# Loading the mLSTM heads' stabilizer rows into buffers of their own, at the start of each head's products

## The chip, the core and the metric

The kernel runs on one core of a Trainium2 chip. The metric is the device time of one execution in microseconds (us), the median of the runs shown; lower is better. Inputs and weights are float32; every product of a weight matrix is made of three passes on TensorE (high part by high part, high by low, low by high), so that one "group" below means three matmuls.

## The reference, cut to what matters

The reference is a block of attention, retention and memory attention with a conv-FFN, followed by a second block of two layers: an mLSTM layer with a multi-scale pool branch (256 positions, 4 heads of 256), and a latent attention layer. The change is in the mLSTM layer. Per head, the chunkwise form of the reference is the same as a form over all 256 positions:

```
i_pre, log_f = gates                       # per head and position
cum = cumsum(log_f)
m   = running maximum of (i_pre - cum), at least 0      # the stabilizer row, 256 numbers per head
s[t, j] = (q_t . k_j) * exp(i_pre_j - cum_j - m_t)      # for j <= t
num = s @ v;  den = sum(s)
h = num / max(|den|, exp(-(cum + m))) * sigmoid(om)
h = rms_norm(h) * gain;  ya = (h + skip * xc) * silu(zm)
yb = pool branch
x + concat(ya, yb) @ w_out
```

## The kernel before

The kernel is one long stream of products on TensorE with its order written by hand; the instructions of the other engines are put into their queues by a planner that goes by program order and data dependences. Weights come in chunks: a DMA on SyncE's queue into one of three `raw` buffers, a cast to the high part `wh` on ScalarE (L370), the low part `wl` by subtraction on VectorE (L374), eight buffers each. A cast may run at most some 70 to 84 matmuls ahead of TensorE (`ahead`, L317).

Beside the products run generators, one per head. `tick()` advances every active generator to its next `yield`. `gemm_pair` ticks after each 8 groups (so twice), `om_product` twice, `narrow_product` and `qkv` once, `kstep` once (8 groups). `later(gen)` puts a generator into a waiting list, from which a tick takes one while fewer than two are active (`WIDTH`); `urgent(gen)` makes it active at once. So the number of yields of a generator fixes behind which product its own matmuls stand in TensorE's queue.

The mLSTM layer starts with the norm (`norm2`, urgent) and then has this order (L1359 to L1398): x, gate, output-gate and z products of head 0; `conv_in(0)`; `gate_rows` (urgent: the gates, the running maximum `mrow`, its DMA to DRAM `m_d`, and after six yields a transpose that gives `na`); products of head 1; `qkv(0)`; z of head 1; one bare `tick()`; `pool_products(0)` (two `gemm_pair`); `qkv(1)`; `om`, z and x products of head 2 with `conv_in(2)` after its x product; `out_steps(0)`, `out_steps(1)`; `tick()`; `qkv(2)`; `pool_products(1)`; products of head 3; `out_steps(2)`; `qkv(3)`; `out_steps(3)`; `pool_products(2)` and `(3)`; `out_steps(4)`, `(5)`; `drain()`; `ktail`. `qkv(h)` ends with `later(mlstm(h))`.

`out_steps(i)` multiplies one piece of `ya` or `yb` with the output weights, two `kstep` each, in the order of `AO_ORDER`: a0, b0, b1, a1, a2, b2; the last two pieces, a3 and b3, are done in `ktail`, tile pair by tile pair (a3 twice, b3 twice, for each pair). `out_steps` first ticks until its piece is ready. A piece a*h* is ready when `mlstm(h)` has ended.

`mlstm(h)` (L1241): wait for the gates; load `m_d`'s row of head h into `e[:, 0:256]` of all partitions (a DMA of GpSimd's queue, L1247); two yields; two VectorE steps that add `na` and the mask (L1250, L1252) and the exponential (L1253); two yields; the score product `sp` (L1256 to L1261) and its multiplication with `e` (L1262); one yield; the value products `np_` (L1267 to L1271), denominators, output gate, norm (L1273 to L1287); eight yields; the four transposes of the result (L1291, by the helper at L626); `y` (L1296, L1298) and its split into high (L417) and low (L421). The pool branch `pool(g)` is a generator too, with three yields and then its `pair_block` product of 4 groups.

Of the kernel before, what the change touches and what calls it, by code (L numbers as in the profile page):

```python
# [8 lines left out]
F32 = mybir.dt.float32  # L9
# [3 lines left out]
ALU = mybir.AluOpType  # L13
# [4 lines left out]
P = 128  # L18
# [205 lines left out]
def build(ctx, tc, aps, ch, wpar, wcon, out):  # L224
    nc = tc.nc
    V, A, PE = nc.vector, nc.scalar, nc.tensor
    E = ctx.enter_context
    cpool = E(tc.tile_pool(name="cpool", bufs=1))
# [8 lines left out]
    def nm(s):  # L237
        count[0] += 1
        return f"{s}_{count[0]}"
# [24 lines left out]
    def lo512(t):  # L264
        return t[:, 0:512]
# [4 lines left out]
    def sm(n, tag="sm", dt=F32, bufs=8):  # L270
        return small.tile([P, n], dt, tag=tag, name=nm(tag), bufs=bufs)
# [6 lines left out]
    def ps_product():  # L278
        product_tags.append(product_tags.pop(0))
        return ps(product_tags[-1])  # L280
# [22 lines left out]
    def C(name):  # L303
        g, o, n = wcon[name]
        return held[g][:, o:o + n]
# [94 lines left out]
    def mm3(out_, l, r, start, stop):  # L400
        mm(out_, l[0], r[0], start, False)
        mm(out_, l[0], r[1], False, False)
        mm(out_, l[1], r[0], False, stop)
# [408 lines left out]
    for u in range(4):  # L812
        nc.sync.dma_start(v3(lo512(TB[u])),
                            bass.AP(tensor=tb_d.tensor, offset=tb_d.offset + 127 + u * 2 * P * 385,
                                    ap=[[384, P], [P * 385, 2], [1, 256]]))
# [83 lines left out]
    for mult in (2.0 ** 14, 1.0):  # L899
# [4 lines left out]
        for n in range(4):  # L904
            if n < 3:
                m, e_ = np.frexp(rest)
# [12 lines left out]
    for w_ in range(2):  # L919
        for t in range(2):  # L920
            c_, s_ = cn[:, t * 32:(t + 1) * 32], sn[:, t * 32:(t + 1) * 32]
            for half in range(2):
# [4 lines left out]
                                       op0=ALU.mult, op1=ALU.mult)  # L927
# [173 lines left out]
    H = [dict() for _ in range(4)]  # L1101
# [66 lines left out]
    def pair_block(acc, c, b0, X2):  # L1168

        for j in range(2):  # L1170
            for k in range(2):
                w = c[b0 + k]
                mm3(acc[:, j * 256:(j + 1) * 256], (w[0][:, j * P:(j + 1) * P], w[1][:, j * P:(j + 1) * P]),
                    (X2[0][:, k * 256:(k + 1) * 256], X2[1][:, k * 256:(k + 1) * 256]), k == 0, k == 1)

    def qkv(h):
        c = Chunk(ch["qkv"][h])
        xm, xc = H[h]["xm"], H[h]["xc"]
        for m, n, sc in ((0, "q", 0.0625), (1, "k", 1.0)):
            acc = ps_product()  # L1180
            pair_block(acc, c, m * 2, xc)
            H[h][n] = new()
            A.activation(lo512(H[h][n]), acc, AF.Copy, scale=sc)
        tick()
        acc = ps_product()
        for t in range(2):
            for k in range(2):
                o = k * 256 + t * P
                mm3(acc[:, t * 256:(t + 1) * 256], (xm[0][:, o:o + P], xm[1][:, o:o + P]), c[4 + k], k == 0, k == 1)
        v = new()  # L1190
        vv = v3(v[:, 0:516])
        V.memset(vv[:, :, 256:257], 1.0)
        A.copy(vv[:, :, 0:256], v3(acc))
        H[h]["v"] = v
        free(xc, xm)
        later(mlstm(h))

    gates = {}
    m_d = dpool.tile([4 * 256], F32, name="m_d")

    def gate_rows(acc):
        ga, gb, gc = new(), new(), new()
        g = ga[0:64, 0:256]
        A.copy(g, acc[64:128, 0:256])
        V.tensor_tensor(g, g, acc[0:64, 0:256], op=ALU.add)
        V.tensor_tensor(g, g, N2["r12b"][0:64, 0:256], op=ALU.mult)
        V.tensor_scalar(g, g, G("bif")[0:64], None, op0=ALU.add)
        f = g[32:36]
        one = small.tile([64, 1], F32, tag="one", name="one", bufs=1)
        V.memset(one, 1.0)  # L1210
        t0 = ga[32:36, 256:512]
        V.scalar_tensor_tensor(t0, f, -1.0, f, op0=ALU.mult, op1=ALU.max)
        A.activation(t0, t0, AF.Exp, scale=-1.0)
        A.activation(t0, t0, AF.Ln, bias=one[32:36])
        lf = gb[0:4, 0:256]
        V.scalar_tensor_tensor(lf, f, 0.0, t0, op0=ALU.min, op1=ALU.subtract)
        zero = gb[0:4, 256:512]
        V.memset(zero, 0.0)
        rows = gc[:, 0:256]
        V.memset(rows, 0.0)  # L1220
        cum = gc[0:4, 256:512]
        V.tensor_tensor_scan(cum, lf, zero, 0.0, op0=ALU.add, op1=ALU.add)
        V.tensor_tensor(rows[0:4], g[0:4], cum, op=ALU.subtract)
        mrow = cpool.tile([4, 256], F32, name="mrow")
        V.tensor_tensor_scan(mrow, rows[0:4], rows[0:4], 0.0, op0=ALU.max, op1=ALU.max)
        nc.gpsimd.dma_start(bass.AP(tensor=m_d.tensor, offset=m_d.offset, ap=[[256, 4], [1, 256]]), mrow)
        V.tensor_tensor(rows[32:36], cum, mrow, op=ALU.add)
        for _ in range(6):
            yield
        pt = ps("q")  # L1230
        for t in range(2):
            PE.transpose(pt[:, t * P:(t + 1) * P], rows[:, t * P:(t + 1) * P], C("ident"))
        free(ga, gb, gc)
        p3 = pt[:, 0:256].rearrange("p (t c) -> p t c", t=2)
        na = sm(8, "na", bufs=1)
        emn = sm(8, "emn", bufs=1)
        V.tensor_scalar(na.rearrange("p (t c) -> p t c", t=2), p3[:, :, 0:4], -1.0, None, op0=ALU.mult)
        A.activation(emn.rearrange("p (t c) -> p t c", t=2), p3[:, :, 32:36], AF.Exp, scale=-1.0)
        gates.update(na=na, emn=emn)

    def mlstm(h):  # L1241
        while not gates:
            yield
        na, emn = gates["na"], gates["emn"]
        d_ = H[h]
        e = new()
        nc.gpsimd.dma_start(e[:, 0:256], bass.AP(tensor=m_d.tensor, offset=m_d.offset + 256 * h, ap=[[0, P], [1, 256]]))  # L1247
        yield
        yield
        V.scalar_tensor_tensor(e[:, 256:384], e[:, 128:256], na[:, 4 + h:5 + h], C("mmask")[:, 0:128],  # L1250
                               op0=ALU.add, op1=ALU.add)
        V.scalar_tensor_tensor(e[:, 0:256], e[:, 0:256], na[:, h:h + 1], C("mmask"), op0=ALU.add, op1=ALU.add)  # L1252
        A.activation(e[:, 0:384], e[:, 0:384], AF.Exp, scale=-1.0)  # L1253
        yield
        yield
        sp = ps("q")  # L1256
        qx, kx = ([d_[n][:, i * 256:(i + 1) * 256] for i in range(2)] for n in "qk")
        for i in range(2):
            mm(sp[:, 0:256], kx[i][:, 0:128], qx[i], i == 0, i == 1)
        for i in range(2):  # L1260
            mm(sp[:, 256:384], kx[i][:, 128:256], qx[i][:, 128:256], i == 0, i == 1)  # L1261
        V.tensor_tensor(e[:, 0:384], e[:, 0:384], sp[:, 0:384], op=ALU.mult)  # L1262
        yield
        hs = new()
        ss = sm(2, "su")
        vv = v3(d_["v"][:, 0:516])
        for t in range(2):  # L1267
            np_ = ps("q")
            mm(np_[:, 0:257], e[:, t * P:(t + 1) * P], vv[:, 0, 0:257], True, t == 0)
            if t:  # L1270
                mm(np_[:, 0:257], e[:, 256:384], vv[:, 1, 0:257], False, True)  # L1271
            den, dcol = sm(1, "den"), sm(1, "dcol")
            V.tensor_copy(dcol, np_[:, 256:257])  # L1273
            V.scalar_tensor_tensor(den, dcol, -1.0, dcol, op0=ALU.mult, op1=ALU.max)
            V.tensor_tensor(den, den, emn[:, 4 * t + h:4 * t + h + 1], op=ALU.max)
            V.reciprocal(den, den)
            hst = hs[:, t * 256:(t + 1) * 256]
            V.scalar_tensor_tensor(hst, np_[:, 0:256], den, d_["om"][:, t * 256:(t + 1) * 256],
                                   op0=ALU.mult, op1=ALU.mult)
            q = new()  # L1280
            A.activation(q[:, 0:256], hst, AF.Square, accum_out=ss[:, t:t + 1])
            free(q)
        free(e)
        r = rsqrt(mean_eps(ss, 2, 256), 2)
        for t in range(2):
            hst = hs[:, t * 256:(t + 1) * 256]
            V.tensor_scalar(hst, hst, r[:, t:t + 1], None, op0=ALU.mult)  # L1287
        for _ in range(4):
            yield
            yield  # L1290
        pt = transposes(hs, (0, 256, 128, 384), "q")  # L1291
        free(hs)
        y = new()
        for i in range(2):
            k = 2 * h + i
            V.scalar_tensor_tensor(y[:, i * 256:(i + 1) * 256], pt[:, i * 256:(i + 1) * 256], G("hg", k),  # L1296
                                   d_["sxc"][:, i * 256:(i + 1) * 256], op0=ALU.mult, op1=ALU.add)
        V.tensor_tensor(lo512(y), lo512(y), lo512(d_["z"]), op=ALU.mult)  # L1298
        split(tuple(lo512(t[h]) for t in YA_t), lo512(y), 0.5)
        free(y, d_["q"], d_["k"], d_["v"], d_["om"], d_["z"], d_["sxc"])  # L1300
        ready.add(("a", h))
# [265 lines left out]
    for t in range(2):  # L1567
        src, d_, tb_ = hd(lo512(qr[t]), 8), hd(lo512(qro[t]), 8), new()
# [86 lines left out]
```

## Time and profile before

| | us |
|---|---|
| median of 3 runs | 799.11 (799.09 to 800.63) |
| the profiled execution | 797.75, of which the span of the instructions is 796.0 |
| TensorE matmuls busy | 779.8 (98%) |
| VectorE busy | 633.9 (80%) |
| ScalarE busy | 471.5 (59%) |
| GpSimd busy | 7.2 (1%) |
| mean granted TensorE clock | 0.993 |

The mLSTM layer takes the stretch from some 470 to 680 us. In the chain of work that ended last, TensorE has 86% of the span and VectorE 8%. Line 398 is the helper that issues every matmul, line 374 the low part of the weights, lines 417, 419 and 421 the split of an operand. The tile name `s` stands for any of the 52 shared work buffers, so lines tell steps apart better than tiles.

### The profile page before, as it was taken

What the parts mean: (1) busy time and instruction counts of PE and PEld (TensorE: products, weight loads), DVE (VectorE), ACT (ScalarE), POOL (GpSimd) and SP (SyncE); (2) the same over time, 40 slices, a digit from 0 to 9 for tenths busy, and PEclk for the clock granted to TensorE, in tenths of its full rate; (3) what the DMA queues carried; (4) which work ended last, traced back from release to release, by engine and by line L of the source; (5) the groups of instructions that cost most, each with busy time, mean ns of one, the idle gap of its engine ahead of it and who ended that gap; (6) DMA issues with size and microseconds to landing.
All of it is one profiled execution on the core that took longest, in us unless ns stands there. A gap on an engine that the chain in (4) does not pass through costs nothing.

```text
span 796.0 us, 15480 instructions
## 1 busy us (share of the span) xinstructions
PE 779.8 (98%) x6078; PEld 757.6 (95%) x6078; DVE 633.9 (80%) x1590; ACT 471.5 (59%) x974; POOL 7.2 (1%) x17
## 2 busy tenths in 40 slices
PE   8999999999999999999999999998999998999998
PEld 7999998999999999999999999998999997998897
DVE  6877588687578799878877898997778796899682
ACT  6474675544545467656556586865546453687770
POOL 1000000000000000000000000000000000001000
PEclk9999999999999999999999999999999999999999
DMA  8787245354455545555555433475435442553301
GB/s 299 224 328 272 102 168 193 106 194 178 159 180 196 198 168 164 208 184 189 207 184 199 170 140 119 160 269 192 166 115 190 173 153 91 201 185 112 154 2 53
DMA packets 25752, 138.20 MB, mean 174 GB/s; under 512 B 3020, under 2 KB 6608, under 8 KB 11856
## 3 DMA queue, kind: packets, MB, share of 16 engines
q1 hardware_dynamic: 25456, 136.70, 48.6%
q0 software_dynamic: 224, 0.53, 0.4%
q8 instruction: 47, 0.77, 0.4%
q14 instruction: 25, 0.20, 0.1%
HBM read 134.59 MB, written 2.63 MB: 172 GB/s over the span
## 4 chain that ended last, share of the span: by engine, by line
PE 86%; DVE 8%; DMA 3%; ACT 1%; issue 1%; SPq 0%; DVEq 0%; ACTq 0%
PE ps_k L398 44%; PE ps_acc L398 26%; PE ps_q L398 14%; DVE wl L374 3%; DMA raw<-in_w_qm_dram 2%; PE ps_acc L626 1%; DMA raw<-in_w_va_dram 1%; DVE s L1117 1%; DMA raw<-in_w_qa_dram 1%; ACT wh L370 1%; DVE s L419 0%; PE ps_q L1532 0%; DVE s L1372 0%; ACT s L417 0%; DVE s L421 0%
## 5 line engine op out<-in xcount | busy, mean ns | idle before, releaser
L398 PE MATMUL ps_k<-s,wh 128*128 128x256 f32 x1888 | 349.8, 287 | 7.9 <-ACT s L417 5.4
L374 DVE TENSOR_TENSOR wl<-raw,wh 128x384 fp32r<-128x384 f32 (+3 forms) x488 | 317.0, 682 | 16.3 <-ACT wh L370 16.2
L398 PEld LDWEIGHTS ps_k<-s,wh 128*128 128x128 f32 x1888 | 295.8, 192 | 10.5 <-ACT s L417 5.8
L370 ACT CAST wh<-raw 128x384 fp32r<-128x384 f32 (+3 forms) x488 | 269.3, 614 | 20.3 <-DMA raw<-in_w_cz_dram 5.5
L398 PE MATMUL ps_k<-s,wl 128*128 128x256 f32 x936 | 266.1, 284 | 1.2 <-DVE wl L374 1.2
L398 PE MATMUL ps_acc<-s,wh 128*128 128x256 f32 x1056 | 190.3, 282 | 1.2 <-DVE s L419 0.8
L398 PEld LDWEIGHTS ps_k<-s,wl 128*128 128x128 f32 x936 | 179.3, 192 | 1.8 <-DVE wl L374 1.8
L398 PEld LDWEIGHTS ps_acc<-s,wh 128*128 128x128 f32 x1056 | 162.6, 189 | 2.0 <-DVE s L419 1.0
L398 PE MATMUL ps_acc<-s,wl 128*128 128x256 f32 x528 | 148.6, 281 | 0.3 <-DVE wl L374 0.3
L398 PEld LDWEIGHTS ps_acc<-s,wl 128*128 128x128 f32 x528 | 99.7, 189 | 0.5 <-DVE wl L374 0.5
L398 PE MATMUL ps_q<-s,wh 128*128 128x256 f32 (+1 forms) x432 | 76.7, 281 | 0.0
L417 ACT ACTIVATE s<-s 128x256 fp32r<-128x256 f32 (+1 forms) x58 | 28.3, 491 | 69.1 <-DVE s L985 18.9
L398 PEld LDWEIGHTS ps_q<-s,wh 128*128 128x128 f32 (+1 forms) x432 | 65.8, 188 | 0.0
L398 PE MATMUL ps_k<-wh,s 128*128 128x512 f32 (+1 forms) x204 | 60.4, 368 | 0.0
L398 PE MATMUL ps_q<-s,wl 128*128 128x256 f32 x208 | 58.5, 281 | 0.0
L1026 ACT ACTIVATE s<-s,par 128x256 f32<-128x256 f32 x44 | 24.0, 594 | 43.3 <-DVE s L1021 43.3
L398 PEld LDWEIGHTS ps_k<-wh,s 128*128 128x128 f32 x204 | 36.4, 189 | 5.5
L398 PEld LDWEIGHTS ps_q<-s,wl 128*128 128x128 f32 x208 | 39.3, 189 | 0.0
L398 PE MATMUL ps_q<-s,s 128*128 128x256 f32 (+3 forms) x190 | 37.6, 337 | 0.0
L398 PE MATMUL ps_acc<-wh,s 128*128 128x256 f32 (+1 forms) x152 | 36.9, 324 | 0.0
L398 PE MATMUL ps_k<-wl,s 128*128 128x512 f32 (+1 forms) x102 | 36.5, 358 | 0.0
L398 PEld LDWEIGHTS ps_q<-s,s 128*128 128x128 f32 x190 | 29.5, 191 | 2.2
(251 smaller groups left out, 756.7 us busy)
## 6 DMA issues: line engine op xcount, KB each, us to landing
raw<-in_w_up_dram SPq DMA_DIRECT2D x22, 1024.0 KB, 4.8
raw<-in_w_dn_dram SPq DMA_DIRECT2D x11, 1024.0 KB, 4.7
raw<-in_w_zar_dram SPq DMA_DIRECT2D x8, 1024.0 KB, 4.8
raw<-in_w_ao_dram SPq DMA_DIRECT2D x8, 1024.0 KB, 4.8
raw<-in_w_br_dram SPq DMA_DIRECT2D x8, 768.0 KB, 4.3
raw<-in_w_zm_dram SPq DMA_DIRECT2D x4, 1024.0 KB, 4.8
raw<-in_w_wo_dram SPq DMA_DIRECT2D x4, 1024.0 KB, 4.8
raw<-in_w_xm_dram SPq DMA_DIRECT2D x4, 1024.0 KB, 4.8
```

Of the source, the lines that this page charges most:

```text
L370: ahead(AHEAD_A - STEP * ((o + f) // 512), A.copy(wh[:, f:g_], raw[:, o + f:o + g_]))
L374: ahead(AHEAD_V, V.tensor_tensor(wl[:, f:g_], raw[:, o + f:o + g_], f32(wh[:, f:g_]), op=ALU.subtract))
L398: products.append(PE.matmul(out_, lhsT=l, rhs=r, start=start, stop=stop, skip_group_check=True).ins)
L417: A.activation(hi, src, AF.Copy, scale=1.0 if scale is None else scale)
L626: PE.transpose(pt[:, i * P:(i + 1) * P], src[:, o:o + P], C("ident"))
L1026: A.activation(cs, u[:, s, 2:258], AF.Identity, scale=G("cw2", o), bias=G("cb", o))
L1117: V.scalar_tensor_tensor(cs, u[:, i, tap:tap + 256], G(f"aw{tap}", o), cs, op0=ALU.mult, op1=ALU.add)
```

## The change

The load of the head's row is issued at the start of `qkv(h)`, before its q product, into a buffer `mr` of its own, of which there are two. `mlstm(h)` begins with the two VectorE steps, which read that buffer and write `e`; the load and the two yields after it are gone from its chain. The running maximum `mrow` no longer has a buffer of its own and is written over `lf`, which has been read by then.

```diff
     def qkv(h):
         c = Chunk(ch["qkv"][h])
         xm, xc = H[h]["xm"], H[h]["xc"]
+        H[h]["m"] = m_ = sm(256, "mr", bufs=2)
+        nc.gpsimd.dma_start(m_, bass.AP(tensor=m_d.tensor, offset=m_d.offset + 256 * h, ap=[[0, P], [1, 256]]))
...
-        mrow = cpool.tile([4, 256], F32, name="mrow")
+        mrow = lf
         V.tensor_tensor_scan(mrow, rows[0:4], rows[0:4], 0.0, op0=ALU.max, op1=ALU.max)
...
         e = new()
-        nc.gpsimd.dma_start(e[:, 0:256], bass.AP(tensor=m_d.tensor, offset=m_d.offset + 256 * h, ap=[[0, P], [1, 256]]))
-        yield
-        yield
-        V.scalar_tensor_tensor(e[:, 256:384], e[:, 128:256], na[:, 4 + h:5 + h], C("mmask")[:, 0:128],
+        m_ = d_["m"]
+        V.scalar_tensor_tensor(e[:, 256:384], m_[:, 128:256], na[:, 4 + h:5 + h], C("mmask")[:, 0:128],
                                op0=ALU.add, op1=ALU.add)
-        V.scalar_tensor_tensor(e[:, 0:256], e[:, 0:256], na[:, h:h + 1], C("mmask"), op0=ALU.add, op1=ALU.add)
+        V.scalar_tensor_tensor(e[:, 0:256], m_, na[:, h:h + 1], C("mmask"), op0=ALU.add, op1=ALU.add)
         A.activation(e[:, 0:384], e[:, 0:384], AF.Exp, scale=-1.0)
```

## Rows read from the trace of the kernel before

**Rows 1.** Waits of TensorE's matmuls, whole span: engine line, releaser: us, times, longest.
```profile
PE ps_k L398 <- ACT s L417: 5.4, 2, 3.0
PE ps_acc L398 <- DVE s L419: 0.8, 1, 0.8
```
**Rows 2.** Windows: stretch, us, busy of PE, PEld, DVE, ACT, POOL; clock, DMA.
```profile
505.00:512.00 7.00, 6.18 (x50) 5.77 (x49) 7.00 (x18) 6.82 (x16) 0.57 (x1) 1.00 0.33 97
548.70:557.38 8.68, 5.34 (x31) 4.90 (x30) 6.85 (x14) 4.97 (x10) 0.00 (x0) 0.80 0.36 124
662.74:669.50 6.76, 4.06 (x21) 3.63 (x20) 3.01 (x5) 2.70 (x5) 0.00 (x0) 0.75 0.05 21
```
**Rows 3.** Timeline of TensorE, first gap: start, us, line, tiles, idle before.
```profile
543.00 0.40 PE L398 MATMUL ps_k<-s,wh 128*128 128x256 f32 x2
...
548.70 0.60 PE L626 MATMUL ps_q<-base,s 128*128 128x128 f32 x4
552.30 0.39 PE L398 MATMUL ps_k<-s,wh 128*128 128x256 f32 x1 [3.00 <-ACT s L417]
...
557.38 1.47 PE L398 MATMUL ps_q<-s,s 128*128 128x256 f32 x8
```
**Rows 4.** Timeline of TensorE, second gap and the wait shortly before it.
```profile
658.44 0.39 PE L398 MATMUL ps_acc<-s,wh 128*128 128x256 f32 x1 [0.76 <-DVE s L419]
...
662.74 0.60 PE L626 MATMUL ps_q<-base,s 128*128 128x128 f32 x4
...
669.50 0.39 PE L398 MATMUL ps_k<-s,wh 128*128 128x256 f32 x2
```
**Rows 5.** Timeline of VectorE after the transposes of the second gap.
```profile
663.38 0.88 DVE L1296 SCALAR_TENSOR_TENSOR s<-ps_q,par,s 128x256 f32<-128x256 f32 x2 [1.05 <-PE ps_q L626]
664.29 0.69 DVE L1298 TENSOR_TENSOR s<-s,s 128x512 f32<-128x512 f32 x1
665.67 0.69 DVE L421 SCALAR_TENSOR_TENSOR s<-s,s 128x512 fp32r<-128x512 f32 x1 [0.69 <-ACT s L417]
```
**Rows 6.** Timeline of TensorE: from head 2's transposes to the second group after them.
```profile
618.54 0.60 PE L626 MATMUL ps_q<-base,s 128*128 128x128 f32 x4
...
619.33 0.28 PE L398 MATMUL ps_k<-s,wh 128*128 128x256 f32 x1
```
**Rows 7.** Timeline of TensorE: gate transposes and head 0's score products.
```profile
508.32 0.38 PE L1232 MATMUL ps_q<-base,s 128*128 128x128 f32 x2
...
517.61 1.47 PE L398 MATMUL ps_q<-s,s 128*128 128x256 f32 x8
```
**Rows 8.** Timeline of VectorE and ScalarE: head 0's steps up to the scores.
```profile
509.44 0.16 DVE L1237 TENSOR_SCALAR na<-ps_q 128x8 f32<-128x8 f32 x1
510.26 0.58 ACT L1183 ACTIVATE s<-ps_k 128x512 f32<-128x512 f32 x1
510.91 0.35 DVE L1250 SCALAR_TENSOR_TENSOR s<-s,na,s 128x128 f32<-128x128 f32 x1
511.92 0.48 DVE L1252 SCALAR_TENSOR_TENSOR s<-s,na,s 128x256 f32<-128x256 f32 x1
512.43 0.53 ACT L1253 ACTIVATE s<-s 128x384 f32<-128x384 f32 x1
519.41 0.55 DVE L1262 TENSOR_TENSOR s<-s,ps_q 128x384 f32<-128x384 f32 x1
```
**Rows 9.** Timeline of GpSimd: the rows' store, the first load, what follows the loads.
```profile
502.29 0.66 POOL L1226 DMA_DIRECT2D m_d<-mrow  x1 [499.31 <-DVE mrow L1225]
505.64 0.57 POOL L1247 DMA_DIRECT2D s<-m_d  x1 [2.69 <-DVE s L1117]
...
719.99 0.52 POOL L672 MEMSET s<- 64x512 f32 x1 [108.91 <-DVE rst L467]
```
**Rows 10.** VectorE's wait for head 3's load; landing times of store and first load.
```profile
615.49 0.35 DVE L1250 SCALAR_TENSOR_TENSOR s<-s,na,s 128x128 f32<-128x128 f32 x1 [3.08 <-DMA s<-m_d]
...
DMA to landing us min/median/max: 2.8/3.0/3.1
```

## The prediction

> **What bounds the kernel now.** I read the page's busy shares first, then TensorE's waits, then the two places that they name. TensorE is busy nearly throughout, so an edit to the mLSTM heads, whose steps run on VectorE, ScalarE and GpSimd, can only gain where TensorE stands still for one of them. The waits show two such places of any size: two waits of 5.4 us together for the high split at L417, the longest 3.0 us, and one of 0.8 us for a low split at L419 [rows 1]. The timeline puts the first at 549: four transposes at 548.70, then nothing until 552.30, and the next product of another kind at 557.38 [rows 3]. The second lies at 662.74 to 669.50 [rows 4]. Both begin with the transposes of an mLSTM head (L626), and the products behind them are the output products of that very head, a0 and a3: TensorE waits while VectorE makes `y` (0.88 us for two L1296, 0.69 us for L1298), ScalarE splits it, and VectorE makes the low part (0.69 us) [rows 5]. The windows show a second loss at both: the granted clock is 0.80 over 8.68 us and 0.75 over 6.76 us, that is 2.4 GHz with a piece at 1.2 GHz just after the standstill [rows 2]. The lost clock is 0.20 x 8.68 = 1.74 us and 0.25 x 6.76 = 1.69 us.
>
> **What the two places cost.** A group of three matmuls at full clock takes (548.70 - 543.00) / 16 = 0.356 us, since an x product of 16 groups fills that time [rows 3]. Head 2's transposes, which stand between other products, take with one group 619.33 - 618.54 = 0.79 us [rows 6]. The first place holds transposes and 8 groups: 0.79 + 7 x 0.356 = 3.28 us without a stall, against 557.38 - 548.70 = 8.68 us; lost 5.40 us. The second holds transposes and 5 groups up to 669.50: 0.79 + 4 x 0.356 = 2.21 us against 6.76 us; lost 4.55 us. Together 9.95 us, the clock included.
>
> **Why those heads stall, by ticks.** I number the ticks from the first after the urgent norm: 7 for head 0's products, 4 for om and x of head 1, tick 12 in `qkv(0)`, 13 and 14 in z of head 1, 15 the bare one, 16 to 19 `pool_products(0)`, 20 `qkv(1)`, 21 to 26 om, z and x of head 2, and so on to 59, the last step of `out_steps(5)`. The six yields of the gates put their transposes behind tick 13. Head 0 starts at 13, loads, passes 14, does its exponential at 15, passes 16, has its scores at 17, its values at 18, and its transposes at 26, which is the end of head 2's x product; `out_steps(0)` follows at once. Heads 1 to 3 start at 23, 33 and 46 and have their transposes at 36, 46 and 59. Tick 59 is the last before `ktail`, whose first item is a3. The rows agree: gate transposes at 508.32, scores at 517.61, which is half a z product and one pool product later, 24 groups or 8.5 us [rows 7], transposes at 548.70 [rows 3] and 662.74 [rows 4] with output products right behind, but at 618.54 with other work behind [rows 6].
>
> **The change part by part.** *Two yields go.* Every later step of a head moves two ticks ahead: head 0's scores to 15, values to 16, transposes to 24; heads 1, 2 and 3 keep their starts (23 and 33 are set by a free place among two active generators, 46 by `qkv(3)`) and have transposes at 34, 44 and 57. Between tick 24 and a0's products now stands the whole x product of head 2, 16 x 0.356 = 5.7 us; between 57 and `ktail` stand b2's two steps, again 5.7 us, and a pool product of 4 groups. What has to be done behind the transposes took 666.36 - 663.38 = 3.0 us from the start of L1296 to the end of L421 [rows 5], so 2.7 us are over for queueing. Both stalls should go whole: -9.95 us. Heads 1 and 2 did not stall and gain nothing.
>
> *What is late next at the first place.* The fourth accumulator of a0's step takes the bank that `conv_in(2)` has to empty, a VectorE step of the size of L1298 (0.69 us, [rows 5]); it is needed only at the seventh group, 6 x 0.356 = 2.1 us in. No cost.
>
> *What is late next at the second place.* Pool 3's product stands between b2's two steps, and TensorE already waits 0.76 us for its split [rows 4]. Head 3's tail, 0.88 + 0.69 + 0.69 = 2.26 us of VectorE [rows 5], now comes into the stretch before that split, while its norm chain leaves the stretch. The transposes, which now stand ahead, give about 0.79 - 0.36 = 0.43 us of cover. Bounds: the whole wait goes, -0.76 us; or the whole tail stands ahead of the split, +2.26 - 0.43 = +1.8 us. The planner can as well put the tail in place of weight casts, so neither end is near; I take about the middle, +0.5 us.
>
> *Head 0's steps come earlier into a full stretch.* From 505 to 512 VectorE is busy 7.00 of 7.00 us and TensorE 6.18 [rows 2], so here VectorE sets the pace. L1250 and L1252 already run there (510.91 and 511.92); L1262, 0.55 us, comes in [rows 8]. The other side is that the scores (1.47 us, [rows 7]) now stand ahead of the pool's product and give the weight casts that time. Bounds: +0.55 + 0.48 = +1.0 us if L1252 and L1262 go ahead of a cast that TensorE waits for; -0.82 us if the 7.00 - 6.18 us of waiting there were all covered. I take 0, as cover and extra work are of one size.
>
> *The chain to the scores and values.* Head 0's scores would stand near 517.61 - 5.7 = 511.9; they need k, copied by 510.26 + 0.58 = 510.84 [rows 8]. The values come 1.47 + 2.85 = 4.3 us later, at 516.2; L1262 can end by 511.9 + 1.47 + 0.55 = 513.9, and the exponential ends at 512.96 even where it was [rows 8]. So 2.3 us are over.
>
> *The loads.* Five DMAs of GpSimd before and after. The store lands at 502.29 + 2.8 = 505.1 and the first load was issued at 505.64 [rows 9, 10], so head 0's load is at most half a microsecond sooner; it lands 3.0 us after its issue, at about 508.1, ahead of `na` at 509.44 [rows 8]. The third and fourth load have to wait until L1252 of heads 0 and 1 has read the buffer. Behind them on GpSimd's queue stand only the memsets at 719.99 [rows 9]: no cost. VectorE's standstill of 3.08 us for head 3's load [rows 10] goes; TensorE has no wait there, so this frees VectorE alone: 0.
>
> *`mrow` over `lf`.* Same scan, same engine, in order; the buffer is given back at tick 13 (508.3), after the store has landed: 0.
>
> Sum in the profiled execution's own time: 797.75 - 9.95 + 0.5 = 788.3 us. The median of the runs is 1.36 us above that execution; the difference carries over: 799.11 - 9.45 = 789.7 us.
>
> The SBUF page speaks against loads from this queue in such a stretch: the Trainium skill (SBUF — State Buffer, "two separate sides") says that GpSimd can't write a DMA's descriptors while a two-port VectorE step holds their shared port. By that rule the load issued at 505 would hang until VectorE pauses. The first load, issued inside the full stretch, landed after 3.0 us, so the trace does not bear it out.
>
> **Rivals.** *Only part goes.* If head 3's tail holds up pool 3's split by the full 1.8 us, the wait there is 2.6 us, as long as the shorter wait for L417 (5.4 - 3.0 = 2.4 us, [rows 1]), and a piece of low clock would follow as it did there (1.69 us): 799.11 - 9.95 + 1.8 + 1.7 = 792.7. If the second stall stays whole, 799.11 - 5.4 = 793.7. For it: VectorE is on the chain before 658. Against: the tail's steps wait for ScalarE between them (0.69 us idle before L421, [rows 5]), so the pool's steps fit in.
>
> *The change doesn't do what it says.* If the stall at 549 came from VectorE's queue (`conv_in(2)` stands before L1296 there) and not from the tick, it would stay, 799.1 within 0.2%. Against: heads 1 and 2 have the same tail and no wait.
>
> *Slower: the values become the place that waits.* The two yields also covered the chain L1250, L1252, L1253, L1262, which now has three ticks (8.6 us; head 0 some 7) from a head's start to its values in TensorE's queue. Its own work is 0.35 + 0.48 + 0.53 + 0.55 = 1.91 us [rows 8]. If queues on VectorE and ScalarE hold it up by more than some 5 us, TensorE stands still at the values of all four heads; at the price of the second place, 4 x 4.55 = 18.2 us, the time would be 799.11 - 9.95 + 18.2 = 807.4. Against: from `na` to the end of the exponential head 0 took 509.44 to 512.96, 3.5 us, in the fullest stretch.
>
> *The load is starved.* As a mechanism of this kernel: head 0's load held back until VectorE itself stands at L1250, then 3.0 us to land; TensorE waits as long and loses clock as at the second place, 3.0 + 1.7: 789.7 + 4.7 = 794.4. The rule of the SBUF page named above would act so.
>
> **How the numbers follow.** Both stalls go: 0.73, at 789.7, its own range 787.6 (-9.95 - 0.76 - 0.82) to 792.0 (-9.95 + 1.8 + 1.0). Part goes: 0.12. Starved load: 0.02. Nothing moves: 0.06. Slower: 0.07. The range 787.6 to 795.0 holds the first three. A measurement of this kernel tells about 0.2% (1.6 us) from no change. Faster 0.87, same 0.06, slower 0.07.
>
> **What would show it.** Right: transposes of L626 right before head 2's x product and before b2's first step, no wait for L417 behind them, no stretch of low clock near 553 or 667; VectorE without a wait for the load. Wrong: TensorE waiting for L1262 at the values, a wait for the pool's L419 above 2 us near 650, or new waits for `wl` between 505 and 520.

## The result, and the profile after

The changed kernel takes 786.98 us (median of 4 runs, 786.61 to 787.36) against 799.10 us (4 runs, 798.48 to 800.63): a ratio of 0.9846 with a 95% interval of 0.9831 to 0.9860, 12.1 us faster. The forecast was 789.7 us with a range of 787.6 to 795.0 us: the direction and the mechanism held, the gain was larger than the range allowed. The profiled execution has a span of 785.3 us at a granted clock of 0.998, where the one of before had 796.0 us at 0.993.

The page's busy line of the kernel after, and TensorE's waits over its whole span (engine line, releaser: us, times, longest), to be read against [rows 1]:

```profile
PE 775.4 (99%) x6078; PEld 753.6 (96%) x6078; DVE 632.1 (80%) x1590; ACT 471.3 (60%) x974; POOL 7.2 (1%) x17
```
```profile
PE ps_k L398 <- ACT wh L370: 2.5, 2, 2.3
PE ps_acc L398 <- DVE s L584: 1.2, 1, 1.2
PE ps_k L398 <- DVE wl L374: 1.2, 3, 0.6
PE ps_acc L398 <- ACT s L523: 0.5, 1, 0.5
PE ps_q L398 <- DVE me L507: 0.3, 1, 0.3
PE ps_q L398 <- DVE s L516: 0.2, 1, 0.2
```

The waits for L417 and L419 are gone, and with them two of 0.7 us together for L421. What is left lies ahead of the mLSTM layer (most of it in the first 28 us), but for the 0.60 us for a weight near 508 and a wait in a norm of the next layer. The chain of work that ended last, in order of time (start, us, what), shows it better still: from 540 to 670 us it is TensorE alone.

```profile
539.90 3.43 PE ps_acc L398 x29
543.33 0.43 PE ps_q L626 x4
543.77 2.85 PE ps_k L398 x24
546.62 1.31 PE ps_q L398 x8
547.93 2.84 PE ps_k L398 x24
550.77 1.30 PE ps_q L398 x6
552.07 11.42 PE ps_k L398 x96
...
643.89 5.66 PE ps_k L398 x48
649.55 0.44 PE ps_q L626 x4
649.98 2.85 PE ps_k L398 x24
652.84 1.44 PE ps_acc L398 x12
654.27 14.40 PE ps_k L398 x120
```

Head 0's transposes (L626) at 543.33 have two half x products, head 1's scores and head 1's values between them and a0's products at 552.07; head 3's at 649.55 have b2's first step, pool 3's product and b2's second step before `ktail`. In the windows (as in [rows 2]) the stretches that answer to the two places have a full TensorE and the full clock:

```profile
543.17:551.80 8.63, 8.63 (x69) 8.39 (x67) 7.22 (x15) 3.56 (x7) 0.00 (x0) 1.00 0.35 124
644.00:657.00 13.00, 13.00 (x113) 13.00 (x112) 12.73 (x24) 5.69 (x11) 0.00 (x0) 1.00 0.43 150
657.00:664.00 7.00, 7.00 (x61) 7.00 (x60) 5.26 (x10) 3.02 (x7) 0.00 (x0) 1.00 0.31 109
```

Where the time went is read by laying the two matmul streams side by side. Both have 6078 matmuls; only those of the heads stand at other places. Start of matmul n, counted from 0, in the two profiled executions, us:

| n | before | after | before minus after | what lies in between |
|---|---|---|---|---|
| 3900 | 500.58 | 501.29 | -0.71 | the first 70 us: the first weights came later in this execution |
| 4200 | 538.51 | 538.67 | -0.16 | head 0's scores: +0.55 |
| 4500 | 580.41 | 575.17 | 5.24 | the first place: +5.40 |
| 5100 | 653.32 | 648.44 | 4.88 | -0.36: most of it ahead of head 3's q |
| 5250 | 677.02 | 666.35 | 10.67 | the second place and the pool's wait: +5.79 |
| last | 791.90 | 781.23 | 10.67 | nothing |

So the mLSTM layer gave 11.38 us, of which 10.67 show in the spans because the start of this execution was 0.71 us later. Of the -0.36 us, 0.26 stand at one place, the first product of head 3's q, whose weight load waits for an accumulator to be copied out:

```profile
609.69 0.19 PEld L398 LDWEIGHTS ps_acc<-wh,s 128*128 128x128 f32 x1 [0.20 <-ACT s L1185]
```

The same count in the other profiles tells the layer from the start. From matmul 3900 to 5250 the kernel before takes 176.44 us, the changed kernel 165.07 us, and 165.05 us in its second profile. The start of matmul 3900 varies with the execution, whatever the kernel: 500.58 us in the profile of before, 500.96 to 502.65 us in the eleven others of this case.

### The profile page after: what moved, and what is told of

The parts are those of the page before. It is cut to its first block, busy times and chain, and to the rows that moved or that the text cites. A ratio compares the mean times of both kernels' runs of the same rounds, so it can differ in the third digit from the quotient of the medians.

```text
span 785.3 us, 15483 instructions
## 1 busy us (share of the span) xinstructions
PE 775.4 (99%) x6078; PEld 753.6 (96%) x6078; DVE 632.1 (80%) x1590; ACT 471.3 (60%) x974; POOL 7.2 (1%) x17
## 4 chain that ended last, share of the span: by engine, by line
PE 91%; DVE 4%; DMA 3%; ACT 1%; SPq 0%; issue 0%; DVEq 0%; ACTq 0%
PE ps_k L398 48%; PE ps_acc L398 28%; PE ps_q L398 14%; DMA s<-in_mem_dram 2%; DVE wl L374 1%; PE ps_acc L626 1%; DMA raw<-in_w_qa_dram 1%; DVE s L1117 1%; PE ps_q L1532 0%; ACT wh L370 0%; DVE s L1372 0%; DVE s L490 0%; ACT s L417 0%; PE ps_q L626 0%; DVE s L421 0%
## 5 line engine op out<-in xcount | busy, mean ns | idle before, releaser
L398 PE MATMUL ps_k<-s,wh 128*128 128x256 f32 x1888 | 345.1, 285 | 2.5 <-ACT wh L370 2.5
L398 PEld LDWEIGHTS ps_k<-s,wh 128*128 128x128 f32 x1888 | 292.3, 190 | 4.6 <-ACT wh L370 3.6
L398 PEld LDWEIGHTS ps_k<-s,wl 128*128 128x128 f32 x936 | 177.4, 190 | 2.2 <-DVE wl L374 2.1
L417 ACT ACTIVATE s<-s 128x256 fp32r<-128x256 f32 (+1 forms) x58 | 28.3, 492 | 64.2 <-DVE s L985 18.9
```

The costliest lines, as they stand in the source:

```text
L398: products.append(PE.matmul(out_, lhsT=l, rhs=r, start=start, stop=stop, skip_group_check=True).ins)
L417: A.activation(hi, src, AF.Copy, scale=1.0 if scale is None else scale)
```

## The experiments

The theory: the gain comes from where the heads' transposes stand in TensorE's queue, two ticks earlier, so that other products cover their tail (the steps from L1296 to L421 that make the operand of the next product out of them). The main rival: it comes from the load, which is now early and for which VectorE no longer stands still.

**The loads early, the yields kept.** The changed kernel with

```diff
         m_ = d_["m"]
+        yield
+        yield
         V.scalar_tensor_tensor(e[:, 256:384], m_[:, 128:256], ...
```

> The changed kernel with the two yields put back between the reading of the buffer and the rest of the chain, so that the loads stay early and in buffers of their own, but every head's transposes stand behind ticks 26, 36, 46 and 59 again. Theory (the place of the transposes in TensorE's queue is the whole gain): both standstills come back, two waits for L417 of about 3.0 and 2.4 us with low clock behind them, and the pool's wait of 0.76 us; 798 to 800 us. Rival (the load, and VectorE standing still 3.1 us for it, was what cost): the time stays near 787 us.

Measured: 799.53 us (12 runs) against 799.26 us (17 runs of the kernel before), ratio 1.0002 (0.9993 to 1.0012). TensorE's waits are those of before, but that the one near 512 for the low part of a weight (the last line) is 0.7 us where it had 0.3:

```profile
PE ps_k L398 <- ACT s L417: 5.4, 2, 3.0
...
PE ps_acc L398 <- DVE s L419: 0.8, 1, 0.8
PE ps_acc L398 <- DVE wl L374: 0.7, 1, 0.7
```

The early loads alone gain nothing; `mrow` over `lf`, which is in this kernel too, neither.

**The yields out, the loads kept in the chain.** The kernel before with

```diff
         nc.gpsimd.dma_start(e[:, 0:256], bass.AP(tensor=m_d.tensor, ...
-        yield
-        yield
```

> The kernel before with only the two yields taken out: the load stays in the head's chain and in its work buffer. Theory: TensorE's order is that of the changed kernel, VectorE still waits some 3 us for a load where it has slack, and TensorE waits only if the load of a head holds up its values; 787 us, up to 790 if VectorE's standstill is handed on. Rival (the early load is what gains): 799 us.

Measured: 791.41 us, ratio 0.9905 (0.9891 to 0.9919), above the 787 to 790 us expected. Both standstills are gone, but a new one has come. Timelines of TensorE, VectorE, ScalarE and GpSimd in the profiled execution, around head 3's load:

```profile
602.89 0.54 POOL L1247 DMA_DIRECT2D s<-m_d  x1 [45.80 <-ACT s L1157]
608.74 0.35 DVE L1248 SCALAR_TENSOR_TENSOR s<-s,na,s 128x128 f32<-128x128 f32 x1 [2.78 <-DMA s<-m_d]
609.70 0.52 ACT L1251 ACTIVATE s<-s 128x384 f32<-128x384 f32 x1 [4.98 <-DVE s L1250]
611.69 1.07 ACT L1183 ACTIVATE s<-ps_acc 128x512 f32<-128x512 f32 x2
612.32 0.39 PE L398 MATMUL ps_acc<-wh,s 128*128 128x256 f32 x1 [2.97 <-ACT s L1183]
```

VectorE stands at its queue's head for the load, ScalarE stands at the exponential for VectorE, and behind the exponential in ScalarE's queue is the copy of head 3's q, which has to empty an accumulator before TensorE can go on. In the kernel before the same standstill of VectorE (3.08 us, [rows 10]) reached no such product. So the theory holds for the two places, and half of the rival comes true in another way: without the yields, which were the load's cover, the load has to be early.

**One head at a time.** The changed kernel with the yields put back for the other three heads:

```diff
         m_ = d_["m"]
+        if h != 0:      # and in a second kernel: h != 3
+            yield
+            yield
```

> The changed kernel with the two yields put back for heads 1, 2 and 3 only. Theory: the first standstill goes (5.40 us by the windows, 5.2 us by the shift of the products between the two traces), the second and the pool's wait stay; 793.5 to 794 us. Rival (the two standstills are not separate, the first one's time comes back at the second): 799 or 787 us.

Measured: 792.78 us, ratio 0.9919 (0.9906 to 0.9932), 6.5 us of gain and 0.7 us below the range expected. In the profile matmuls 3900 to 5250 take 5.76 us less than before.

> The changed kernel with the two yields put back for heads 0, 1 and 2 only. Theory: the first standstill stays, the second goes (4.55 us) and with it the pool's wait of 0.76 us; 793.3 to 794.5 us. If the pool's wait went only because of something that head 0's earlier chain does, it stays and the time is 0.8 us more.

Measured: 793.70 us, ratio 0.9932 (0.9920 to 0.9945), 5.6 us of gain; the pool's wait for L419 is gone in its profile, and the same matmuls take 5.39 us less. The two add up to 12.0 us by the medians, each known to about 1 us, against 12.1 for the whole change, and to 11.15 us by the matmuls, against 11.37 (176.44 - 165.07). So the places are independent within that, and heads 1 and 2 gain nothing. The 0.36 us ahead of head 3's q are lost in neither of the two profiles.

**Head 3's load alone early.** As the kernel without yields and with loads in the chain, but

```diff
     def qkv(h):
+        if h == 3:
+            H[h]["m"] = m_ = sm(256, "mr", bufs=1)
+            nc.gpsimd.dma_start(m_, ...row 3 of m_d...)
...
-        V.scalar_tensor_tensor(e[:, 0:256], e[:, 0:256], na[:, h:h + 1], ...
+        V.scalar_tensor_tensor(e[:, 0:256], m_, na[:, h:h + 1], ...   # m_ is e[:, 0:256] for heads 0 to 2
```

> The kernel before without the two yields, loads of heads 0 to 2 in the chain, and only head 3's load moved to the start of its products, into a buffer of its own. Theory (with the yields gone, the one load that hurts is head 3's: VectorE stands for it, ScalarE stands behind VectorE at the exponential, and the copy of head 3's q, which empties an accumulator, comes late): the wait of 3.0 us for L1183 goes; the time of the changed kernel, 787 to 788 us. Rival (the early loads of the other heads matter too, or the wait comes from somewhere else): 789 to 791.5 us.

Measured: 787.76 us, ratio 0.9843 (0.9830 to 0.9856), the changed kernel's time; matmuls 3900 to 5250 take 165.05 us, as there. Of the four early loads one is needed.

**How much cover is enough.** The changed kernel with one yield put back:

```diff
         m_ = d_["m"]
+        yield
```

> The changed kernel with one yield put back, so that the transposes stand behind ticks 25, 35, 45 and 58. Theory (cover against tail): at the first place half an x product (8 groups, 2.85 us) is left ahead of a0's products, against a tail of 3.0 us plus what VectorE and ScalarE have queued, so TensorE waits there between 0.2 and 1.5 us, too short for a piece of low clock; at the second place the pool's product and one step of b2 (4.3 us) are left and hide it; 787.2 to 788.7 us. Rival (a standstill is all or nothing, its clock with it): 792 us.

Measured: 788.22 us, ratio 0.9863 (0.9849 to 0.9878). The time is in the range expected, but the wait that was to make it is not there: TensorE doesn't wait for the tail at all, so nothing here shows what so short a wait would do to the clock. I had left out that head 1's scores also stand between. Timeline of TensorE, from head 0's transposes on, with head 1's scores and values:

```profile
547.79 0.60 PE L626 MATMUL ps_q<-base,s 128*128 128x128 f32 x4
...
551.06 1.47 PE L398 MATMUL ps_q<-s,s 128*128 128x256 f32 x8
...
555.32 1.03 PE L398 MATMUL ps_q<-s,s 128*128 128x257 f32 x4
```

VectorE's L421 for this head ended at 552.45 (551.76 + 0.69), the scores at about 552.2: the tail is just hidden.

```profile
548.43 0.88 DVE L1297 SCALAR_TENSOR_TENSOR s<-ps_q,par,s 128x256 f32<-128x256 f32 x2 [1.21 <-PE ps_q L626]
...
551.76 0.69 DVE L421 SCALAR_TENSOR_TENSOR s<-s,s 128x512 fp32r<-128x512 f32 x1
```

**Only the transposes moved.** Two yields back early in the chain, two of the eight late ones out:

```diff
         m_ = d_["m"]
+        yield
+        yield
...
-        for _ in range(4):
+        for _ in range(3):
             yield
             yield
         pt = transposes(hs, (0, 256, 128, 384), "q")
```

> The changed kernel with the two yields put back early in the chain and two of the eight late yields taken out instead: scores and values stand where they stood before, only the transposes keep their new place (24, 34, 44, 57). Theory: nearly all of the gain is here, 787 to 788 us; 0.5 us of wait for a weight's low part near 512 comes back, because head 0's scores no longer stand ahead of the pool's product. For the pool's wait near 650: if it goes here too, the transposes ahead of it and not the norm chain's earlier place took it away; if it stays (0.8 us) it was the norm chain. Rival (scores and values had to move as well): 790 us or more.

Measured: 788.23 us, ratio 0.9863 (0.9848 to 0.9878). All waits for a tail are gone, the pool's too, and the wait near 512, gone in the changed kernel, is back:

```profile
512.88 0.39 PE L398 MATMUL ps_acc<-s,wl 128*128 128x256 f32 x1 [0.69 <-DVE wl L374]
```

So the transposes' place is nearly the whole gain, and the pool's wait went because of them, not because the norm chain had moved.

**Two ticks more.** The changed kernel with `range(3)` in place of `range(4)` alone:

> The changed kernel with two of the eight late yields taken out, transposes at 22, 32, 42 and 55. Theory: TensorE has no wait for a head's tail left, so more cover is worth nothing: 787.0 us within 0.5. If it is slower, the norm chain no longer fits between the values and the transposes (six ticks, 17 us).

Measured: 788.15 us, ratio 0.9862 (0.9848 to 0.9877): a little slower than expected, for a reason I had not named. Head 3's tail now falls at the start of pool 3's chain, and nothing stands in front of the pool's product that would cover it. VectorE's steps of the tail (L1296, L1298, L421) lie among those of the pool (L1311, L1317), and TensorE waits again, for the pool's split. By the matmuls the second place gains 4.30 us here and 5.78 us in the changed kernel; in return the 0.36 us ahead of head 3's q are not lost. Waits over the whole span, then VectorE's timeline:

```profile
PE ps_acc L398 <- DVE s L419: 0.7, 1, 0.7
...
PE ps_acc L398 <- ACT s L417: 0.2, 1, 0.2
```
```profile
643.69 0.69 DVE L1311 TENSOR_TENSOR s<-ps_acc,s 128x512 f32<-128x512 f32 x1 [0.17 <-PE ps_acc L398]
644.30 0.87 DVE L1296 SCALAR_TENSOR_TENSOR s<-ps_q,par,s 128x256 f32<-128x256 f32 x2
645.08 0.71 DVE L1317 TENSOR_TENSOR s<-s 128x542 f32<-128x542 f32 x1
645.71 0.68 DVE L1298 TENSOR_TENSOR s<-s,s 128x512 f32<-128x512 f32 x1
646.31 0.71 DVE L1317 TENSOR_TENSOR s<-s 128x538 f32<-128x538 f32 x1
```

**The scaling of x later.** The changed kernel with the eight steps of L1372 moved from before the bare `tick()` to behind `pool_products(0)`, which was meant to take away the last wait of the layer:

> The changed kernel with the eight steps that scale x (L1372, 0.48 us each) moved behind the first pool products, out of the stretch in which VectorE sets the pace. Theory: the wait of 0.60 us for a weight's low part near 508 goes and nothing replaces it; 786.4 us. If those steps were filling gaps only, no change: 787.0 us.

Measured: 787.63 us, ratio 0.9852 (0.9836 to 0.9869). The wait of 0.60 us is still there, and matmuls 3900 to 5250 take 165.04 us, no less than in the changed kernel; those steps delay nothing that TensorE waits for. No version here is faster than the changed kernel.

**The changed kernel again.**

> The changed kernel once more beside the kernel before on the same chip, for the share of the gain that the profiled executions don't show: 10.7 us between the two profiled spans, 12.1 us between the medians. If the kernel before loses clock at its standstills in most executions beyond the profiled one (0.993 granted there), its executions spread by a few us along their granted clock and those of the changed kernel don't; 786.5 to 788.3 us, ratio 0.984 to 0.987.

Measured: 787.17 us against 799.59 us (9 runs), ratio 0.9841 (0.9827 to 0.9854). The kernel before varies along its granted clock; over the 33 executions of it that stood beside the experiments:

| granted clock | executions | median span, us |
|---|---|---|
| 0.993 or 0.994 | 7 | 796.8 |
| 0.991 | 24 | 797.7 |
| 0.989 | 2 | 799.1 |

The changed kernel's eight executions have spans from 784.5 to 785.9 us at 0.996 to 0.998. The profiled execution of before that the prediction worked from, 796.0 us at 0.993, is shorter than any of the 33.

## Why the prediction was right in kind and short in size

- **The two standstills.** Right: with their causes (the ticks), their places and their size. First place, 5.40 us predicted, 5.40 us in the shift of the matmuls; second place 4.55 us predicted, 4.8 us (5.79 less the pool's 1.0). Heads 1 and 2 gained nothing, as said. The cover was more than the 5.7 us I counted at the first place, as head 1's scores and values stand there too. Not counted were the 0.36 us lost ahead of head 3's q.
- **The pool's wait.** The term that was mis-sized most: +0.5 us, the middle of -0.76 and +1.8, where all of it went. The transposes ahead of pool 3's product gave it cover, and the planner put only L1296 among the pool's last steps, and L1298 and L421 behind the pool's split (L419). The bound was too small as well: the profile gives 0.76 us idle [rows 4], but the product's first two matmuls, 657.30 and 658.44, start 1.14 us apart where they start 0.12 us apart elsewhere, so 1.0 us was to be had. Row of before (timeline of TensorE); then the split and the step behind it after (VectorE), and the same product after:

```profile
657.30 0.39 PE L398 MATMUL ps_acc<-s,wh 128*128 128x256 f32 x1
```
```profile
651.65 0.68 DVE L419 TENSOR_TENSOR s<-s,s 128x512 fp32r<-128x512 f32 x1
652.25 0.68 DVE L1298 TENSOR_TENSOR s<-s,s 128x512 f32<-128x512 f32 x1
```
```profile
652.67 0.40 PE L398 MATMUL ps_acc<-s,wh 128*128 128x256 f32 x2
652.91 0.29 PE L398 MATMUL ps_acc<-s,wl 128*128 128x256 f32 x1
```

- **Head 0's steps in the full stretch.** Predicted 0, measured a gain of 0.55 us. Cover and extra work were not of one size: the scores ahead of the pool's product gave the casts 1.3 us, and L1262, though among the casts, delayed none that TensorE waited for. The wait near 512 returns (0.7 us) in the four kernels profiled with the yield or yields kept for head 0 and the loads early.
- **The loads and GpSimd's queue.** No cost, as said. The first load was issued at 505.64 and 505.65 in the two kernels. (The 3.0 us given for its landing before is the middle of the store's 2.8 and the load's own 3.1.) I had put VectorE's standstill for head 3's load at 0; in the kernel before that was right, but with the yields gone it would have cost TensorE 3.0 us, which the prediction did not see because it priced the yields and the early load one by one.
- **From the profiled execution to the median.** The step that put the time out of the range. "The difference carries over" is true only if the profiled executions of both kernels lie alike among their runs. That of before was shorter than any of the 33 others: the earliest start of the twelve profiles, 0.71 us ahead of the changed kernel's, at a granted clock of 0.993, where 26 of the 33 had 0.991 or less. That of after was an average one, 0.1 us above its median where that of before was 1.36 us below. The medians differ by 1.4 us more than the spans, 12.1 against 10.7 us. With the layer's terms right, 9.45 would have been 11.4 us and the forecast 787.7 us, still in the range; this step took the measured time out of it. Half of the 1.4 us is the start, 0.71 us. The other half goes with the lower clock of most executions of before; where in them that clock was lost stays open, as none of those was profiled.
- **The rivals.** "Only part goes" fell with the pool's wait; "the change doesn't do what it says" fell, as moving the transposes alone took both stalls away; "slower" fell, the values wait for nothing in any kernel without the yields. The starved load did not show either: the first three loads were issued in a stretch where VectorE was busy throughout (7.70 of 7.70 us) and landed 3.2 to 3.3 us later, the fourth 5.3 us. So none of the first three waited for a pause of VectorE. What the Trainium skill says (SBUF — State Buffer, "two separate sides") is of VectorE steps in a two-port mode. The prediction took the whole full stretch for such steps without a row that shows it, so these landings neither bear the rule out nor speak against it.

```profile
505.00:512.70 7.70, 7.10 (x57) 6.84 (x57) 7.70 (x20) 7.45 (x17) 1.54 (x3) 1.00 0.38 106
```

## What to carry to other kernels

Where side chains are threaded through a hand-ordered queue, count at which product each of their matmuls lands; a stall whose product follows its own transposes was cured here by moving them a product earlier, by a step that the chain could spare. A yield that is taken out was cover for something: move that something (here one DMA) ahead in the same edit. Price a standstill by start-to-start times rather than by idle time alone, and before a difference between two spans is carried to a median, see where the profiled execution lies among its runs.

## What was not expected of the hardware

A standstill of TensorE is not followed by low clock in every execution. In the kernel before, the waits of 3.00 and 2.36 us were both followed by a piece of it (0.80 and 0.75 granted, [rows 2]). The kernel with the loads in the chain has one standstill of 2.97 us in its layer, and its profiled execution kept the full clock behind it (window as in [rows 2]):

```profile
612.30:620.00 7.70, 7.68 (x64) 7.68 (x65) 4.33 (x8) 5.61 (x11) 0.00 (x0) 1.00 0.54 167
```

That execution had 0.998 over its span of 788.0 us; two others had 0.996 and 789.5 and 789.6 us, and two 0.993 and 790.4 and 790.7 us. That these four lost their clock behind the standstill is not shown, as they were not profiled. It can also be lost at the start: from 1 to 20 us the granted clock is 0.91 in nine of the twelve profiles and 0.82 in three (head 3 alone, one yield, head 3's load alone early), and those three reach matmul 3900 last, at 502.02 to 502.65 us. The Trainium skill (TensorE: Matmul & The Clock Gate, "What's actually happening") says that the number of matmuls at the low clock at a kernel's start differs from run to run of one kernel. The start here agrees in that it has two values, 0.91 and 0.82, though over twelve executions of eleven kernels.
